# Hybrid decoder layer on one core: the head of its z stage with a plain fp32 first product

## The chip, the cores and the metric

The kernel runs on one core of a Trainium2 chip. A core has a matrix engine (PE, with PEld for its weight loads), a vector engine (DVE), a scalar engine (ACT), a general engine (POOL), and SyncE (SP), which issues most of the transfers. Each engine works through its own list of instructions in order and waits on semaphores for the others. Matrix products are written to PSUM, a small memory of banks; everything else works in SBUF. The metric is the device time of one execution in microseconds, the median of several.

## The reference

One decoder layer with 1024 tokens of 1024 features in fp32. Cut to what matters here:

```python
h = rms_norm(x, norm1_w)                       # x * rsqrt(mean(x*x) + 1e-6) * norm1_w
proj = h @ w_in                                # 1024 x 3592
da_q, da_k, da_v, dn_qkv, dn_z, dn_a, dn_b = split(proj)
...                                            # differential attention; gated DeltaNet, times silu(dn_z)
x = x + mix @ w_out
h = rms_norm(x, norm2_w)
x = x + square(relu(h @ w_up)) @ w_down
```

The columns of `dn_z` (512), `dn_a` and `dn_b` (4 each) are computed first. They are the 520 columns from 3072 on, and this is what the text calls the z stage.

## The kernel before, in words

The program runs through these stages: norm and z; the DeltaNet's projections with their preparation; its scan together with the attention's projections; attention; output projection; and the two products of the MLP, which use a scheme of seven products in place of eight.

Almost every product is made in three passes. An fp32 operand is split into a rounded part H (type fp32r, which PE reads faster) and the remainder L. Then H·H, H·L and L·H are added up. A split costs one ACT copy (rounding) and one DVE subtraction (remainder). `hH` and `hL` hold the split, normalised and turned input for the whole first half of the program; the function `nat` makes one product from them, 8 blocks of the inner dimension with 3 matmuls each (lines 206, 207 and 208 in `mm3`).

The z stage works on 8 row blocks (`tb`) of 128 tokens and 2 weight units (`u`) of 260 columns. For each row block:

- `z_square` makes the sum of squares on ACT (two halves for block 0), then the root on DVE and POOL (`rstd`, lines 231 and 232).
- `z_scale` multiplies x by the root and by norm1_w on DVE. The row norm1_w was spread over all 128 partitions at the start by a matmul with ones; this is an fp32 matmul without a split.
- `z_turn` transposes 4 of the 8 column blocks on PE into a PSUM tile; `h_round` (ACT) and `h_rest` (DVE) split that tile into `hH` and `hL`.
- `z_mm` is the product with one weight unit, into one of two buffers of the pool `pj`. `z_gate` reads it: tanh on ACT, a multiply on DVE (L300), a multiply with the norm weight on POOL, a store. The DVE instruction is the last reader of the PSUM buffer for unit 0.

Each weight unit comes in four raw quarters `wraw` of 260 KB. `z_round` (ACT) and `z_rest` (DVE) split one quarter. The transfers stand on SP in the order of the text: x of block 0 in two halves, the four quarters of unit 0, x of block 1, the four quarters of unit 1, a norm weight, x of blocks 2 to 7.

In the z stage the order of PE, DVE and ACT is written out by hand (`manual_schedule`). The first four products are block 0 with unit 0, block 1 with unit 0, block 0 with unit 1 and block 1 with unit 1. As `pj` has two buffers, the third product waits until the gate has read the first. In the hand order that gate stands behind the splits of both units and behind the root of block 2. All other order, and that of SP and POOL, is set by a scheduler; a planner with costs for each engine (`Interleave`) arranges later stages.

Of the kernel before, what the change touches and what calls it, by code (L numbers as in the profile page):

```python
# [13 lines left out]
ALU = mybir.AluOpType  # L14
# [107 lines left out]
def tile_hymba_layer(  # L122
# [140 lines left out]
    def z_unit(u):  # L263

        ops = [staged(t).rearrange("p (k c) -> p k c", k=KB) for t in ("wH", "wL")]
        raws = []
        for k in range(0, KB, 2):
            raw = n1.tile([P, 2 * UC], F32, tag="wraw", name="wraw", bufs=8).rearrange("p (k c) -> p k c", k=2)
            nc.sync.dma_start(raw, w_in_v[:, k:k + 2, 3072 + UC * u:3072 + UC * (u + 1)])
            raws.append(raw)  # L270
        return ops, raws

    xts = [n1.tile([P, DM], F32, tag="xt", name="xt", bufs=NT) for _ in range(NT)]
    w1r = n1.tile([P, DM], F32, tag="hn", name="w1r", bufs=2)[0:1, :]
    nc.scalar.dma_start(w1r, norm1_w)
    cuts = (slice(0, 512), slice(512, 1024))
    for c in cuts:
        nc.sync.dma_start(xts[0][:, c], x2[0:P, c])
    wz = [z_unit(0)]
    nc.sync.dma_start(xts[1], x2[P:2 * P, :])  # L280
    wz.append(z_unit(1))
    dnw4 = n1.tile([P, 4, P], F32, name="dnw4")
    nc.sync.dma_start(dnw4[:, 0], dn_out_norm_w.partition_broadcast(P))
    for tb in range(2, NT):
# [5 lines left out]
    def z_mm(tb, u):  # L290
        ps = pj.tile([P, 512], F32, tag="pj", name="ps_z")
        nat(ps[:, :UC], tb, wz[u][0], 0, UC)
        return ps

    def z_gate(tb, u, ps):
        n = UC if u == 0 else 252
        th = n1.tile([P, UC], F32, tag="zth", name="zth", bufs=2)
        S.activation(th[:, :n], ps[:, :n], AF.Tanh, scale=0.5)
        zg = n1.tile([P, UC], F32, tag="zg", name="zg", bufs=4)
        last = V.scalar_tensor_tensor(zg[:, :n], th[:, :n], 1.0, ps[:, :n], ALU.add, ALU.mult)  # L300
        G.tensor_tensor(zg[:, :n], zg[:, :n], dnw4[:, UC * u:UC * u + n], ALU.mult)
        if u == 1:
            last = V.tensor_copy(ab[:, tb, :], ps[:, 252:260])
        nc.sync.dma_start(zg_d[tb, :, UC * u:UC * u + n], zg[:, :n])
        return last

    def z_round(u, i):
        S.copy(wz[u][0][0][:, 2 * i:2 * i + 2], wz[u][1][i])

    def z_rest(u, i):  # L310
        wh, wl = [x[:, 2 * i:2 * i + 2] for x in wz[u][0]]
        V.tensor_tensor(wl, wz[u][1][i], wh.bitcast(F32), ALU.subtract)
# [1 line left out]
    hns_, turned_ = {}, {}  # L314

    def z_square(tb, parts=1):

        sq = n1.tile([P, DM], F32, tag="nsq", name="nsq", bufs=1)
        ss = n1.tile([P, 2], F32, tag="nss", name="nss", bufs=2)
        for i in range(parts):  # L320
            c = cuts[i] if parts > 1 else slice(0, DM)
            S.activation(sq[:, c], xts[tb][:, c], AF.Square, accum_out=ss[:, i:i + 1])
# [4 lines left out]
        hns_[tb] = n1.tile([P, DM], F32, tag="hn", name="hn", bufs=2), r  # L327

    def z_scale(tb, c):
        hn, r = hns_[tb]  # L330
        return V.scalar_tensor_tensor(hn[:, c], xts[tb][:, c], r, w1b[:, c], ALU.mult, ALU.mult)

    def z_turn(tb, g):
        ps = pt_.tile([P, 512], F32, tag="pt", name="ps_tr")
        for j in range(4 * g, 4 * g + 4):
            last = T.transpose(ps[:, (j % 4) * P:(j % 4 + 1) * P], hns_[tb][0][:, j * P:(j + 1) * P], ident)
        turned_[tb, g] = ps.rearrange("p (k t) -> p k t", k=4)
        return last

    def h_round(tb, g):  # L340
        return S.copy(hH[:, 4 * g:4 * g + 4, tb * P:(tb + 1) * P], turned_[tb, g])

    def h_rest(tb, g):
        ks, sl = slice(4 * g, 4 * g + 4), slice(tb * P, (tb + 1) * P)
        V.tensor_tensor(hL[:, ks, sl], turned_[tb, g], hH[:, ks, sl].bitcast(F32), ALU.subtract)

    ones = gp.tile([P, P], F32, name="ones")
    with tc.manual_schedule(engines={T.engine, V.engine, S.engine}):


        V.memset(ones, 1.0)
        pw = pm.tile([P, 512], F32, tag="pm", name="ps_w")
        for i in range(6):
            T.transpose(pw[:, 0:P], ident, ident)
        pws = []
        for c in cuts:
            ps = ph.tile([P, 512], F32, tag="ph", name="ps_w1")
            T.matmul(ps, ones[0:1, :], w1r[:, c], start=True, stop=True)
            pws.append(ps)
        for i in range(6):  # L360
            T.transpose(pw[:, 0:P], ident, ident)
        V.tensor_copy(w1b[:, cuts[0]], pws[0])
        z_square(0, 2)
        V.tensor_copy(w1b[:, cuts[1]], pws[1])
        z_round(0, 0)
        for g in range(2):
            z_scale(0, cuts[g])
            z_turn(0, g)
            h_round(0, g)
            if g == 0:  # L370
                z_round(0, 1)
                z_rest(0, 0)
                h_rest(0, 0)
        z_rest(0, 1)
        h_rest(0, 1)
        for i in (2, 3):
            z_round(0, i)
            z_rest(0, i)
        banks0 = {0: z_mm(0, 0)}
        z_square(1)  # L380
        z_scale(1, slice(0, DM))
        z_round(1, 0)
        z_rest(1, 0)
        for g in range(2):
            z_turn(1, g)
            h_round(1, g)
            h_rest(1, g)
            z_round(1, 1 + g)
            z_rest(1, 1 + g)
        banks0[1] = z_mm(1, 0)  # L390
        z_round(1, 3)
        z_rest(1, 3)
# [11 lines left out]
        z_square(3)  # L404
        z_gate(0, 1, banks0[2])
        z_scale(3, slice(0, DM))
        z_gate(1, 1, banks0[3])
        for tb in range(2, NT):
            ps = z_mm(tb, 0)
            if tb + 1 < NT:  # L410
                marks = [z_turn(tb + 1, 0), z_turn(tb + 1, 1)][1:]
                for g in range(2):
                    marks += [h_round(tb + 1, g)]
                    h_rest(tb + 1, g)
            marks += [z_gate(tb, 0, ps)]
            if tb + 2 < NT:
                z_square(tb + 2)
                z_scale(tb + 2, slice(0, DM))
# [1321 lines left out]
```

## Time and profile before

| | |
|---|---|
| median of 3 runs | 1268.11 us (1265.73 to 1270.84) |
| the profiled execution | 1264.09 us, of which the profile's span is 1262.1 us |
| PE busy | 1234.1 us, 98% |
| DVE busy | 817.8 us, 65% |
| ACT busy | 614.0 us, 49% |
| instructions | 18992 |

In the lines that follow, a row of the timeline has the start, the duration, the engine, the line of the kernel, the operation and its tiles, a count, and in brackets the idle time of that engine ahead of it and what ended it. Rows of busy time by windows have their columns named where they stand. Times count from the start of the span. The duration of a matmul in these rows includes its way through the array; matmuls that follow each other start closer together than their duration.

### The profile page before, as it was taken

To read this page: it belongs to the slowest core of one execution; us is meant where nothing else is said; L and a number is where in the kernel's file an instruction comes from. 1 tells how busy PE (TensorE), PEld (TensorE's weight loads), DVE (VectorE), ACT (ScalarE), POOL (GpSimd) and SP (SyncE) were. 2 spreads that over 40 slices of the span, in tenths; PEclk is the share of its full clock that TensorE was granted. 3 is DMA by queue.
4 is the path that set the end of the run, shared out by engine and by line. 5 is a ranking of instruction groups with operands and counts; after the bars stand their busy time and mean duration, and the time that the engine had idled before them with its cause. 6 is when DMAs were issued, how large, how long until landed. Compare 5 with 4: busy or idle time off the path is not lost.

```text
span 1262.1 us, 18992 instructions
## 1 busy us (share of the span) xinstructions
PE 1234.1 (98%) x6973; PEld 1061.5 (84%) x6973; DVE 817.8 (65%) x1416; ACT 614.0 (49%) x1237; POOL 111.0 (9%) x141
## 2 busy tenths in 40 slices
PE   8999999999999999998999999999999999999998
PEld 7988888899998998887887888888887788888887
DVE  6557797557657647776589555665566865687553
ACT  4469554334446545665557444554554333333331
POOL 2211110022212300011200000000000000000000
PEclk9999999999999999999999999999999999999999
DMA  6135554368858656334246534534368755433311
GB/s 240 39 94 144 142 165 118 82 191 260 258 144 245 168 179 162 99 91 143 94 147 207 191 136 167 183 134 144 124 226 323 302 200 200 167 101 100 128 39 67
DMA packets 165814, 200.02 MB, mean 158 GB/s; under 512 B 20905, under 2 KB 126169, under 8 KB 165722
## 3 DMA queue, kind: packets, MB, share of 16 engines
q1 hardware_dynamic: 165720, 198.82, 48.8%
q8 instruction: 55, 0.90, 0.3%
q14 instruction: 37, 0.30, 0.1%
q10 hardware_dynamic: 2, 0.00, 0.0%
HBM read 132.71 MB, written 66.06 MB: 157 GB/s over the span
## 4 chain that ended last, share of the span: by engine, by line
PE 85%; DMA 8%; DVE 3%; ACT 2%; issue 1%; SPq 1%; POOLq 0%; DVEq 0%; POOL 0%; ACTq 0%
PE X L1368 4%; PE X L1367 4%; PE X L1366 4%; PE ps_qk L941 4%; PE ps_qk L942 4%; PE ps_qk L943 4%; PE X L1662 3%; PE X L1663 3%; PE X L1661 3%; PE ps_dn L206 3%; PE ps_dn L207 3%; PE ps_dn L208 3%; PE Y L1366 2%; PE Y L1367 2%; PE Y L1368 2%; PE ps_o L1109 2%
## 5 line engine op out<-in xcount | busy, mean ns | idle before, releaser
L1285 ACT CAST hH<-ur 128x1024 fp32r<-128x1024 f32 x56 | 58.6, 1050 | 175.6 <-PE Z L1662 85.2
L1286 DVE TENSOR_TENSOR hL<-ur,hH 128x1024 fp32r<-128x1024 f32 x56 | 68.3, 1222 | 82.4 <-ACT hH L1285 82.3
L941 PE MATMUL ps_qk<-wH,hH 128*128 128x256 f32 x384 | 114.8, 299 | 0.1
L942 PE MATMUL ps_qk<-wL,hH 128*128 128x256 f32 x384 | 108.5, 283 | 0.0
L943 PE MATMUL ps_qk<-wH,hL 128*128 128x256 f32 x384 | 108.4, 282 | 0.0
L1286 DVE TENSOR_TENSOR op<-raw,op 128x1024 fp32r<-128x1024 f32 x48 | 58.7, 1223 | 74.2 <-PE X L1367 39.5
L1662 PE MATMUL X<-hL,hH 128*128 128x512 f32 x224 | 87.4, 390 | 2.7 <-DVE hL L1286 2.7
L1661 PE MATMUL X<-hH 128*128 128x512 f32 x224 | 87.5, 391 | 1.4 <-DVE b L1563 1.4
L1663 PE MATMUL X<-hH,hL 128*128 128x512 f32 x224 | 87.3, 390 | 0.0
L206 PE MATMUL ps_dn<-hH,wH 128*128 128x512 f32 x192 | 76.2, 397 | 0.3 <-ACT cp L561 0.3
L208 PE MATMUL ps_dn<-hH,wL 128*128 128x512 f32 x192 | 76.0, 396 | 0.0
L207 PE MATMUL ps_dn<-hL,wH 128*128 128x512 f32 x192 | 75.7, 395 | 0.0
L941 PEld LDWEIGHTS ps_qk<-wH,hH 128*128 128x128 f32 x384 | 73.5, 191 | 0.3 <-ACT qn L960 0.2
L942 PEld LDWEIGHTS ps_qk<-wL,hH 128*128 128x128 f32 x384 | 73.5, 191 | 0.0
L943 PEld LDWEIGHTS ps_qk<-wH,hL 128*128 128x128 f32 x384 | 73.2, 191 | 0.0
L1286 DVE TENSOR_TENSOR hL<-dw,hH 128x1024 fp32r<-128x1024 f32 x56 | 68.0, 1217 | 3.2 <-ACT hH L1285 3.2
L1285 ACT CAST op<-raw 128x1024 fp32r<-128x1024 f32 x48 | 50.4, 1052 | 36.9 <-PE Y L1368 19.9
L1285 ACT CAST hH<-dw 128x1024 fp32r<-128x1024 f32 x56 | 58.5, 1047 | 14.8 <-PE Z L1663 8.1
L565 DVE SCALAR_TENSOR_TENSOR cy<-cp,pv,cy 128x512 f32<-128x512 f32 x72 | 53.6, 745 | 13.1 <-ACT cy L563 12.4
L201 DVE TENSOR_TENSOR wL<-wraw,wH 128x512 fp32r<-128x512 f32 x64 | 43.8, 697 | 27.8 <-ACT wH L200 27.5
L200 ACT CAST wH<-wraw 128x512 fp32r<-128x512 f32 x64 | 38.2, 621 | 43.2 <-DMA wraw<-in_w_in_dram 28.5
L1070 ACT ACTIVATE pexp<-ps_sc,mx 128x128 f32<-128x128 f32 (+7 forms) x64 | 47.4, 741 | 22.9 <-DVE mx L1066 22.6
(354 smaller groups left out, 3459.8 us busy)
## 6 DMA issues: line engine op xcount, KB each, us to landing
ur<-ud SPq DMA_DIRECT2D x28, 1024.0 KB, 5.1
raw<-in_w_up_dram SPq DMA_DIRECT2D x32, 512.0 KB, 3.9
dw<-in_w_down_dram SPq DMA_DIRECT2D x32, 512.0 KB, 7.3
wraw<-in_w_in_dram SPq DMA_DIRECT2D x48, 256.0 KB, 2.9
qk_d<-qa SPq DMA_DIRECT2D x32, 256.0 KB, 3.6
ud<-ua SPq DMA_DIRECT2D x16, 512.0 KB, 2.6
ud<-s SPq DMA_DIRECT2D x16, 512.0 KB, 2.7
pka<-park_d SPq DMA_DIRECT2D x32, 192.0 KB, 3.8
```

The source lines that it names most:

```text
L206: T.matmul(ps, lh(k), rh(k), start=(k == 0), stop=False)
L207: T.matmul(ps, lh(k), rl(k), start=False, stop=False)
L208: T.matmul(ps, ll(k), rh(k), start=False, stop=(k == n - 1))
L941: T.matmul(ps[:, :256], hH[:, k, sl], wh[:, k, :], start=(k == 0), stop=False)
L942: T.matmul(ps[:, :256], hH[:, k, sl], wl[:, k, :], start=False, stop=False)
L943: T.matmul(ps[:, :256], hL[:, k, sl], wh[:, k, :], start=False, stop=(k == KB - 1))
L1285: S.copy(dst[0], src)
L1286: V.tensor_tensor(dst[1], src, dst[0].bitcast(F32), ALU.subtract)
L1366: T.matmul(ps, op[0][:, k, cs], h[0][:, k, :], start=start and k == 0, stop=False, skip_group_check=True)
L1661: T.matmul(bank[t], v[0][:, j, sl], v[2][:, j], start=s0, stop=False, skip_group_check=True)
L1662: T.matmul(bank[t], v[0][:, j, sl], v[3][:, j], start=False, stop=False, skip_group_check=True)
L1663: T.matmul(bank[t], v[1][:, j, sl], v[2][:, j], start=False, stop=s1, skip_group_check=True)
```

## The change

Four things change, all in the z stage.

1. The first product (block 0, unit 0) no longer uses the split operands. Block 0's turned tiles are copied whole to a new fp32 tile `hF`, and 8 plain fp32 matmuls multiply `hF` with the raw weight quarters. The split of block 0 into `hH` and `hL` is made later, from `hF`, between the weight splits of unit 1, for the third product.
2. The transfer of x of block 1 is issued ahead of the four quarters of unit 0. Block 1 is squared and scaled early, and its 8 transposes stand between the fourth and the fifth matmul of the first product.
3. The splits of unit 0 are made for the second product; all but the first quarter's stand behind the rounding of block 1.
4. `z_square` is parted into `z_square` (the sum of squares) and `z_root`. The squares themselves, which nobody reads, go into the tile that later holds the scaled x, and their own tile is gone. norm1_w is loaded into a row of `hF`.

```diff
-    w1r = n1.tile([P, DM], F32, tag="hn", name="w1r", bufs=2)[0:1, :]
+    hF = n1.tile([P, KB, P], F32, name="hF")
+    w1r = hF.rearrange("p k c -> p (k c)")[0:1, :]
...
-    wz = [z_unit(0)]
     nc.sync.dma_start(xts[1], x2[P:2 * P, :])
-    wz.append(z_unit(1))
+    wz = [z_unit(u) for u in range(2)]
...
         V.tensor_copy(w1b[:, cuts[0]], pws[0])
         z_square(0, 2)
+        z_root(0, 2)
         V.tensor_copy(w1b[:, cuts[1]], pws[1])
-        z_round(0, 0)
+        z_square(1)
         for g in range(2):
             z_scale(0, cuts[g])
+            if g == 0:
+                z_root(1)
             z_turn(0, g)
-            h_round(0, g)
...
+            S.copy(hF[:, 4 * g:4 * g + 4, :], turned_[0, g])
         z_scale(1, slice(0, DM))
+
+        ps = pj.tile([P, 512], F32, tag="pj", name="ps_z")
+        banks0 = {0: ps}
+        for k in range(KB):
+            if k == 4:
+                z_turn(1, 0)
+                z_turn(1, 1)
+            T.matmul(ps[:, :UC], hF[:, k, :], wz[0][1][k // 2][:, k % 2, :], start=k == 0, stop=k == KB - 1)
+        z_round(0, 0)
+        z_round(0, 1)
+        z_rest(0, 0)
+        for g in range(2):
+            h_round(1, g)
+            h_rest(1, g)
+            z_round(0, 2 + g)
+            z_rest(0, 1 + g)
+        z_rest(0, 3)
         z_round(1, 0)
         z_rest(1, 0)
         for g in range(2):
-            z_turn(1, g)
-            h_round(1, g)
-            h_rest(1, g)
+            ks = slice(4 * g, 4 * g + 4)
+            S.copy(hH[:, ks, 0:P], hF[:, ks, :])
+            V.tensor_tensor(hL[:, ks, 0:P], hF[:, ks, :], hH[:, ks, 0:P].bitcast(F32), ALU.subtract)
             z_round(1, 1 + g)
             z_rest(1, 1 + g)
         banks0[1] = z_mm(1, 0)
         z_round(1, 3)
         z_rest(1, 3)
         z_square(2)
+        z_root(2)
         z_gate(0, 0, banks0[0])
```

More of the change, by code (lines that the diff above doesn't have):

```diff
@@ L316, in z_square @@
     def z_square(tb, parts=1):
-        sq = n1.tile([P, DM], F32, tag="nsq", name="nsq", bufs=1)
+        hn = n1.tile([P, DM], F32, tag="hn", name="hn", bufs=2)
         ss = n1.tile([P, 2], F32, tag="nss", name="nss", bufs=2)
@@ L321, in z_square, with z_root @@
             c = cuts[i] if parts > 1 else slice(0, DM)
-            S.activation(sq[:, c], xts[tb][:, c], AF.Square, accum_out=ss[:, i:i + 1])
+            S.activation(hn[:, c], xts[tb][:, c], AF.Square, accum_out=ss[:, i:i + 1])
+        hns_[tb] = hn, ss
+    def z_root(tb, parts=1):
+        hn, ss = hns_[tb]
         if parts > 1:
@@ L326, in z_square @@
         rstd(r, ss[:, 0:1], 1.0 / DM, EPS, n1, "nrt", 1)
-        hns_[tb] = n1.tile([P, DM], F32, tag="hn", name="hn", bufs=2), r
+        hns_[tb] = hn, r
     def z_scale(tb, c):
@@ L363, in tile_hymba_layer @@
         z_square(0, 2)
+        z_root(0, 2)
         V.tensor_copy(w1b[:, cuts[1]], pws[1])
-        z_round(0, 0)
+        z_square(1)
         for g in range(2):
             z_scale(0, cuts[g])
+            if g == 0:
+                z_root(1)
             z_turn(0, g)
-            h_round(0, g)
[L370 to L380, printed above, removed]
-        z_scale(1, slice(0, DM))
+            S.copy(hF[:, 4 * g:4 * g + 4, :], turned_[0, g])
+        z_scale(1, slice(0, DM))
+        ps = pj.tile([P, 512], F32, tag="pj", name="ps_z")
[14 more added lines that the diff above has]
+        z_rest(0, 3)
         z_round(1, 0)
@@ L404, in tile_hymba_layer @@
         z_square(3)
+        z_root(3)
         z_gate(0, 1, banks0[2])
@@ L417, in tile_hymba_layer @@
                 z_square(tb + 2)
+                z_root(tb + 2)
                 z_scale(tb + 2, slice(0, DM))
```

## The prediction

> **What bounds the kernel now.** I read three views in this order: the page, to see which engine the whole program leans on; busy time by windows, to see where that engine is not full; the timeline of the first 25 us, to see what it waits for there.
>
> ```profile
> span 1262.1 us, 18992 instructions
> PE 1234.1 (98%) x6973; PEld 1061.5 (84%) x6973; DVE 817.8 (65%) x1416; ACT 614.0 (49%) x1237; POOL 111.0 (9%) x141
> ```
>
> PE, the matrix engine, is busy for 98% of the span, so a microsecond that it waits at the head is a microsecond of the kernel, unless a later wait swallows it.
>
> ```profile
> 0.00:5.00 5.00, 3.46 (x9) 2.10 (x10) 0.25 (x3) 2.62 (x5) 1.87 (x11) 1.00 0.57 174
> 5.00:10.00 5.00, 4.34 (x13) 2.07 (x11) 2.88 (x7) 1.26 (x4) 0.55 (x1) 1.00 1.02 333
> ...
> 20.00:25.00 5.00, 4.78 (x40) 4.56 (x40) 4.73 (x8) 2.58 (x6) 1.30 (x2) 1.00 0.21 60
> 25.00:30.00 5.00, 5.00 (x44) 5.00 (x44) 2.58 (x6) 2.78 (x6) 1.97 (x3) 1.00 0.49 160
> 30.00:40.00 10.00, 10.00 (x86) 9.83 (x85) 4.96 (x10) 3.21 (x7) 2.72 (x5) 1.00 0.14 44
> ```
>
> The columns are the stretch, its length, then busy time (and count) of PE, its weight loads, DVE, ACT and POOL, the granted clock, the DMA share and GB/s. From 25 us on PE has no gap (5.00 of 5.00, 10.00 of 10.00). DVE is nearly full in 20 to 25 (4.73 of 5.00). So the question is only when the gapless stretch begins. The timeline has it:
>
> ```profile
> 1.54 1.54 PE L354 MATMUL ps_w<-ident 128*128 128x128 f32 x6 [1.54 <-POOL ident masks.py:199]
> ...
> 6.18 0.62 ACT L308 CAST wH<-wraw 128x520 fp32r<-128x520 f32 x1 [1.17 <-DMA wraw<-in_w_in_dram]
> ...
> 7.43 0.74 DVE L331 SCALAR_TENSOR_TENSOR hn<-xt,nr,w1b 128x512 f32<-128x512 f32 x1
> ...
> 8.22 1.12 PE L336 MATMUL ps_tr<-ident,hn 128*128 128x128 f32 x4
> 9.38 0.59 ACT L341 CAST hH<-ps_tr 128x512 fp32r<-128x512 f32 x1 [2.57 <-PE ps_tr L336]
> ...
> 10.00 0.69 DVE L345 TENSOR_TENSOR hL<-ps_tr,hH 128x512 fp32r<-128x512 f32 x1 [1.22 <-ACT hH L341]
> ...
> 13.18 0.69 DVE L345 TENSOR_TENSOR hL<-ps_tr,hH 128x512 fp32r<-128x512 f32 x1 [1.23 <-ACT hH L341]
> ...
> 14.09 1.05 ACT L322 ACTIVATE nsq<-xt 128x1024 f32<-128x1024 f32 x1
> ...
> 15.27 0.15 DVE L231 TENSOR_SCALAR nrt<-nss 128x1 f32<-128x1 f32 x1
> ...
> 16.12 1.28 DVE L331 SCALAR_TENSOR_TENSOR hn<-xt,nr,w1b 128x1024 f32<-128x1024 f32 x1 [0.70 <-DMA xt<-in_x_dram]
> ...
> 18.22 0.59 ACT L341 CAST hH<-ps_tr 128x512 fp32r<-128x512 f32 x1 [2.46 <-PE ps_tr L336]
> ...
> 18.84 0.69 DVE L345 TENSOR_TENSOR hL<-ps_tr,hH 128x512 fp32r<-128x512 f32 x1 [0.82 <-ACT hH L341]
> ...
> 19.44 0.69 DVE L312 TENSOR_TENSOR wL<-wraw,wH 128x520 fp32r<-128x520 f32 x1
> ...
> 20.05 0.68 DVE L345 TENSOR_TENSOR hL<-ps_tr,hH 128x512 fp32r<-128x512 f32 x1
> ...
> 20.65 1.30 DVE L312 TENSOR_TENSOR wL<-wraw,wH 128x520 fp32r<-128x520 f32 x2
> ...
> 21.95 0.15 DVE L231 TENSOR_SCALAR nrt<-nss 128x1 f32<-128x1 f32 x1
> ...
> 22.23 0.43 DVE L300 SCALAR_TENSOR_TENSOR zg<-zth,ps_z 128x260 f32<-128x260 f32 x1
> ...
> 22.71 0.39 PE L206 MATMUL ps_z<-wH,hH 128*128 128x260 f32 x1 [0.23 <-DVE zg L300]
> ```
>
> The last row is the one that matters. The third product (block 0, unit 1) starts at 22.71 because the accumulators have two buffers and it reuses the first one, which DVE releases by its gate instruction `zg` (L300) at 22.23. From there PE never stops. That gate stands on DVE behind all splits of both weight units. I call the start of the third product S: S before is 22.71, and the change is worth what it moves S by. What PE gains ahead of S, it only waits away.
>
> DVE has the same instructions ahead of that gate in both kernels: three scalings, eight weight remainders (L312), four remainders of h (L345) and the two small root steps of blocks 1 and 2. So S moves only by DVE's idle time between them, of which the rows show 1.22, 1.23, 0.70 and 0.82 us before.
>
> **The change, part by part.** *Up to the first turn* nothing on the path moves: block 0's x still is first in the queue, so DVE scales at 7.43, PE turns at 8.22 and ACT copies at 9.38. That copy now is a plain copy to hF (same 128x512, 0.59). In the old trace the next engine took up such a copy at 10.00, 0.62 after it began. So the first plain product starts at 10.0 instead of behind the splits, for the old one stood at 12.17:
>
> ```profile
> 12.17 0.57 PE L206 MATMUL ps_z<-wH,hH 128*128 128x260 f32 x1
> 12.53 0.42 PE L207 MATMUL ps_z<-wL,hH 128*128 128x260 f32 x1
> 12.75 0.42 PE L208 MATMUL ps_z<-wH,hL 128*128 128x260 f32 x1
> ...
> 16.69 0.28 PE L206 MATMUL ps_z<-wH,hH 128*128 128x260 f32 x1
> 16.81 0.28 PE L207 MATMUL ps_z<-wL,hH 128*128 128x260 f32 x1
> ...
> 17.55 1.07 PE L336 MATMUL ps_tr<-ident,hn 128*128 128x128 f32 x8 [0.34 <-DVE hn L331]
> ```
>
> *Price of the plain product.* Old matmuls follow each other at 0.216 us at first (12.53 to 12.75) and at 0.12 later (16.69 to 16.81), though the clock column says 1.00 throughout: PE runs at half pace until about 16.3, 4.1 us after its first product matmul. The one plain fp32 matmul of this kernel is the broadcast of norm1_w:
>
> ```profile
> L358 PE MATMUL ps_w<-w1r,ones x4: 1056/1056/1217, 3.0 to 5.7; 1*128 1x512 f32 x4
> ```
>
> Two instructions leave four records, 0.90 us apart ((5.7 - 3.0) / 3) for 512 columns at half pace. For 260 columns that is 0.457 a record, and two old sweeps (2 x 0.216) give 0.43: I take 0.44, so 0.88 a matmul, half of it at full pace. Eight take 7.0 us at half pace against 24 x 0.216 = 5.2 for the old product. The first four, ahead of block 1's turn, take 3.5 (3.45 to 3.66): 10.0 to 13.5.
>
> *Turn of block 1 inside the product.* ACT took up a turned group 1.16 us after PE began it at half pace (8.22 to 9.38) and 0.67 after at full pace (17.55 to 18.22). If the pace rises 4.1 us after the first dense matmul, as before, it does so at 14.1, and 0.6 us of the four transposes' 1.12 lie ahead of that. I take 1.1, nearest to the half-pace row: ACT rounds the first group at 14.6 (bounds 14.17 and 14.8). In the old kernel this point is 18.22.
> The Trainium skill, "TensorE: Matmul & The Clock Gate", Part 1, says that the clock starts at half and doubles after one busy window of some 3.4 us. By that the pace would rise at 13.4, ACT would round at 14.2 and S would come 0.4 earlier than mine; the trace's own 4.1 us is used.
>
> *DVE from there.* The first h remainder follows 0.62 later (18.22 to 18.84). Behind it are queued eleven subtractions instead of the old five, because the split of unit 0 is moved behind the turn (only its first quarter lies ahead): four of h and seven of weights. Five took 18.84 to 21.95, 0.622 each; eleven take 6.84. The plain operands hF come from SBUF rather than PSUM; the weight remainders do too, and their rows are as long (0.69), so no extra price. Then 0.28 from the root step to the gate (21.95 to 22.23) and 0.48 from the gate to PE (22.23 to 22.71).
>
> ACT must keep ahead of this:
>
> ```profile
> 18.70 0.63 ACT L308 CAST wH<-wraw 128x520 fp32r<-128x520 f32 x1
> ...
> 19.23 0.59 ACT L341 CAST hH<-ps_tr 128x512 fp32r<-128x512 f32 x1
> ...
> 19.70 1.16 ACT L308 CAST wH<-wraw 128x520 fp32r<-128x520 f32 x2
> ...
> 20.76 1.07 ACT L322 ACTIVATE nsq<-xt 128x1024 f32<-128x1024 f32 x1
> ```
>
> Its copies start 0.51 apart (five in 18.22 to 20.76), faster than DVE's 0.622; ten of them and block 2's square end 6.3 us after the turn (5.1 and the 1.2 of a square with its sum, below), and the tanh 0.4 later, while DVE comes to the gate after 7.74. The two extra ACT copies to hF are ahead of the turn, while ACT has nothing else: nothing. That lead of 1.0 is what hides them; were it gone, every copy more would cost its 0.51.
>
> *Sum:* S = 14.6 + 0.62 + 6.84 + 0.28 + 0.48 = 22.82, against 22.71: +0.1 us (by the bounds of the turn, 14.17 and 14.8, -0.3 to +0.3). DVE begins its chain 3.6 us earlier (15.2 for 18.84) but has six more subtractions in it (3.7 us). The idle time has only moved: DVE now stands still from about 12.2 to 15.2, while the first plain half is computed.
>
> *x of block 1 ahead of the weights.* In the first 5 us 870 kB land (174 GB/s), then 333 kB a us. Both blocks of x (1049 kB) are there at 5.5 by bytes. But the first weight quarter, 790 kB down the old queue and thus due at 4.5, was taken up only at 6.18: a lag of up to 1.6. So block 1 lands between 5.5 and 7.1. Its square and sum take 1.2 (14.09 to 15.27), and its root step stands on DVE between the two scalings of block 0, in a slot at 8.1 (7.43 + 0.66): 6.7 to 8.3 against 8.1, so 0 to 0.2, taken as 0. It costs more beyond that, see below. The first weight quarter (1315 kB) then lands by 6.3 to 7.9, and PE wants it at 10.0: hidden by 2 us. On SP the issue of x goes ahead of four weight issues, all done before their bytes can move; the other issues stay. On POOL the root of block 1 goes ahead of the norm-weight steps, whose result is first needed at the gate: nothing.
>
> *Rest.* Squares written into hn instead of a buffer of their own: hn of that block isn't written before. The root split off from the square has the same neighbours from block 2 on. The order of every engine behind the third product is unchanged, so nothing later moves but by S. All together: 1264.09 + 0.1 = 1264.2 by this execution's own time. The median of the runs shown, 1268.11, is 4.0 higher than it, so my figure for the median is 1268.2.
>
> **Rivals.**
> *Slower: PE falls back to half pace in the new wait.* The turn ends at about 14.7, four more plain matmuls at 0.44 take it to 16.5, and the second product ends at 19.4 (24 x 0.12 = 2.9); then PE waits for the gate until 22.8, 3.4 us, where the old wait is 0.23. Where the pace rises late, the second product ends at up to 21.6 and only 1.2 remain. For it: PE ran at half pace at 12.5 after standing still and turning. Against: no row shows it fall back once full. Price: the third product at 0.216 instead of 0.12, 24 x 0.096 = 2.3 us: 1270.5. It decides once that wait is long enough to count as idle; it could then happen on every execution. The same page and section of the skill put that at an idle window of some 3.4 us that runs free of the kernel; no trace here shows it, and a wait of 3.4 would rarely cover a whole one.
> *Faster: the pace rises inside the first plain half*, because four sweeps without a break count sooner than the old product's first matmuls. At 12.5 the half ends 0.5 earlier and the turn runs at full pace: ACT rounds at 13.7, S = 21.9, 0.8 before the old one: 1267.3. For it: the rise in the old trace isn't tied to a count. Against: 7.8 us of transposes and one-row matmuls from 1.54 on did not raise it.
> *Slower: block 1 lands late.* Its root stands in front of the second scaling, so past 6.9 every us of landing delays the plain product by one: at 8.0 it is +1.1, 1269.3. For it: the 1.6 us lag. Against: x rows came without such a lag.
> *No rise before the second product:* it then takes 5.2 from 18.7 and ends at 23.9; S is 1.2 later: 1269.3. The old rise came 4.1 us into dense work; here 8.7 us lie ahead.
>
> **How the numbers follow.** Forecast 0.60; fall back 0.15; early rise 0.13; late landing 0.06; late rise 0.03; something outside the head 0.03, of either sign. The runs spread from 1265.73 to 1270.84 (0.2% each way), more than any case, so the range is these cases plus the runs: low 1264.09 - 0.8 = 1263.3, high 1270.84 + 0.7 = 1271.5. 0.5% is 6.3 us, about what a measurement of this kernel can tell from no change; no case reaches it, so only the last 0.03 and a part of the fall back (if it repeated) go outside: faster 0.02, same 0.95, slower 0.03.
>
> **What would show it.** The plain product's first record at 10.0, 16 records 0.44 apart at first; ACT's first round of block 1 at 14.6; eleven subtractions on DVE without a gap from 15.2; the second product ended near 19.4 to 21.6 and the third waiting for DVE `zg` until 22.8; full PE from there. It is wrong if PE's third product starts more than 1 us off that, if its first matmuls are 0.216 apart, or if the splits read hF at another price than 0.69.

## The result, and the profile after

The changed kernel takes 1271.02 us in the median of 20 runs (1264.87 to 1278.2) against 1266.85 us for the kernel before (1263.77 to 1270.95, also 20 runs). The ratio is 1.0029, with a 95% interval of 1.0017 to 1.0040. A second set of runs of the same two kernels gave 1.0035 (1.0018 to 1.0052). So the change costs 0.3%, some 4 us: less than the 0.5% within which the prediction had put it, yet a loss that both intervals keep clear of nothing, and forty times the 0.1 us that the prediction's sum had.

The profiled execution of the changed kernel has a span of 1266.2 us and a time of 1267.95 us, 4.1 us of span more than before. The page of the changed kernel, in its lines for the span, the busy time of each engine and three of the DMA queues:

```profile
span 1266.2 us, 18974 instructions
PE 1235.3 (98%) x6965; PEld 1063.1 (84%) x6965; DVE 816.8 (65%) x1416; ACT 615.3 (49%) x1239; POOL 111.2 (9%) x141
...
q1 hardware_dynamic: 165720, 198.82, 48.9%
q8 instruction: 55, 0.90, 0.3%
q14 instruction: 37, 0.30, 0.1%
```

PE is as busy as before, but it has 8 matmuls and 8 weight loads fewer (6965 for 6973 each). The columns of the queue lines are packets, MB and share. Queue 8 carries instructions: 55 packets that are 0.90 MB together, thus 16 kB each. 0.90 MB over PE's 13,930 records are 65 bytes a record, so they are taken here for PE's own program, fetched while it runs, some 250 records at a time. That line was on the page of before too, and the prediction passed over it. Whose instructions queue 14 carries is not shown.

The timeline of the changed kernel's head answers to the prediction's last steps. Only the rows that answer to a step are shown:

```profile
7.50 1.06 ACT L321 ACTIVATE hn<-xt 128x1024 f32<-128x1024 f32 x1 [2.54 <-DMA xt<-in_x_dram]
...
8.68 0.15 DVE L231 TENSOR_SCALAR nrt<-nss 128x1 f32<-128x1 f32 x1 [0.51 <-ACT hn L321]
...
10.39 1.92 PE L385 MATMUL ps_z<-wraw,hF 128*128 128x260 f32 x8
...
12.15 1.04 PE L340 MATMUL ps_tr<-ident,hn 128*128 128x128 f32 x8
12.78 0.59 ACT L345 CAST hH<-ps_tr 128x512 fp32r<-128x512 f32 x1 [0.56 <-PE ps_tr L340]
13.02 1.92 PE L385 MATMUL ps_z<-wraw,hF 128*128 128x260 f32 x8
...
13.40 0.69 DVE L349 TENSOR_TENSOR hL<-ps_tr,hH 128x512 fp32r<-128x512 f32 x1 [0.97 <-ACT hH L345]
...
17.58 0.28 PE L208 MATMUL ps_z<-wH,hL 128*128 128x260 f32 x1
...
20.41 0.14 DVE L231 TENSOR_SCALAR nrt<-nss 128x1 f32<-128x1 f32 x1
20.47 0.41 DVE L300 SCALAR_TENSOR_TENSOR zg<-zth,ps_z 128x260 f32<-128x260 f32 x1
...
20.93 0.58 PE L206 MATMUL ps_z<-wH,hH 128*128 128x260 f32 x1 [3.08 <-DVE zg L300]
...
21.53 0.42 PE L208 MATMUL ps_z<-wH,hL 128*128 128x260 f32 x1
21.75 0.42 PE L206 MATMUL ps_z<-wH,hH 128*128 128x260 f32 x1
...
24.17 0.28 PE L206 MATMUL ps_z<-wH,hH 128*128 128x260 f32 x1
24.29 0.28 PE L207 MATMUL ps_z<-wL,hH 128*128 128x260 f32 x1
```

Half of the plain product takes 1.92 us here, where the prediction had 3.5. The turn of block 1 stands at 12.15, ACT rounds it at 12.78, and the eleven subtractions run from 13.40 to 20.41. The third product, whose start the prediction calls S, begins at 20.93, which is 1.8 us ahead of before. (In four other executions with the same order up to there, S was 21.05 to 21.94.) But PE has stood still for 3.08 us ahead of it, and it then runs at 0.216 a matmul until about 24, when it goes back to 0.12. Busy time by windows of the same kernel shows it in the clock column, the third from the right:

```profile
15.00:20.00 5.00, 2.86 (x24) 2.65 (x22) 5.00 (x9) 4.65 (x10) 0.60 (x2) 1.00 0.98 393
20.00:25.00 5.00, 4.07 (x22) 4.07 (x23) 2.96 (x5) 0.00 (x0) 2.02 (x3) 0.66 0.21 59
```

0.66 is a mean over full and half pace. From 25 us on, the same piece of PE's work stands 0.4 us earlier than before. So in this execution the head has gained, and the whole loss arises later.

Where that is can be worked out by pairing the matmuls of two executions by their order and subtracting their start times. This table is worked out so from the traces (us by which PE is behind before, in the stretch that begins at that time; three of the kernels are experiments of the next section):

```
stretch   after  before_minus8  after_shift8  gate_shift8
  40       -0.4      -0.4           1.6          -1.8
 240       -1.0      -1.2           0.9          -1.9
 260       -0.2      -0.6           0.8          -2.0
 360        0.0       0.3           1.6          -1.7
 380        0.8       1.2           1.7          -1.9
 400        3.4       2.4           3.8          -0.9
 960        1.7       2.6           1.7          -2.5
1000        4.2       4.6           1.2          -4.0
```

The changed kernel loses 0.8 us at 254, 0.8 near 375, 2.7 near 400 (of which 1.7 come back by 660) and 2.4 near 998. None of these places was touched.

Part of such a loss is a longer wait, and part is the half pace that can follow it. The windows near 400 and near 1000 us have it in the clock column; first the kernel before:

```profile
395.00:410.00 15.00, 12.10 (x96) 11.09 (x95) 9.80 (x24) 8.56 (x24) 4.04 (x5) 1.00 0.85 248
990.00:1010.00 20.00, 17.34 (x69) 13.87 (x69) 20.00 (x16) 7.27 (x8) 0.00 (x0) 0.91 0.63 243
```
```profile
395.00:410.00 15.00, 10.77 (x76) 10.17 (x75) 8.51 (x20) 7.17 (x19) 3.64 (x4) 0.89 0.78 240
990.00:1010.00 20.00, 15.78 (x59) 12.52 (x58) 20.00 (x16) 7.05 (x7) 0.00 (x0) 0.83 0.84 314
```

It is not this execution alone. The mean granted clock of a run is 0.997 in the median of 35 runs of the kernel before and 0.994 in 12 of the changed one (the runs of after_again, below). 0.003 of 1265 us is 3.8 us, against 4.6 between their medians. So up to that much of the loss is more time at half pace, and what has to be explained is why PE waits longer and then falls back more often.

### The profile page after: what moved, and what is told of

The parts are those of the page before. It is cut to its first block, busy times and chain, and to the rows that moved or that the text cites. A ratio compares the mean times of both kernels' runs of the same rounds, so it can differ in the third digit from the quotient of the medians.

```text
span 1266.2 us, 18974 instructions
## 1 busy us (share of the span) xinstructions
PE 1235.3 (98%) x6965; PEld 1063.1 (84%) x6965; DVE 816.8 (65%) x1416; ACT 615.3 (49%) x1239; POOL 111.2 (9%) x141
## 4 chain that ended last, share of the span: by engine, by line
PE 86%; DMA 8%; DVE 3%; ACT 1%; SPq 1%; issue 1%; DVEq 0%; POOL 0%; ACTq 0%
PE X L1384 4%; PE X L1383 4%; PE X L1382 4%; PE X L1678 4%; PE X L1679 3%; PE X L1677 3%; PE ps_qk L957 3%; PE ps_dn L206 3%; PE ps_qk L959 3%; PE ps_qk L958 3%; PE ps_dn L208 3%; PE ps_dn L207 3%; PE Y L1384 2%; PE Y L1383 2%; PE Y L1382 2%; DMA wraw<-in_w_in_dram 2%
## 5 line engine op out<-in xcount | busy, mean ns | idle before, releaser
L581 DVE SCALAR_TENSOR_TENSOR cy<-cp,pv,cy 128x512 f32<-128x512 f32 x72 | 53.5, 745 | 11.0 <-ACT cy L579 10.3
L1082 DVE TENSOR_REDUCE mx<-ps_sc 128x1 f32<-128x128 f32 (+7 forms) x64 | 47.6, 754 | 17.2 <-PE ps_sc L1080 17.0
```

## The experiments

Theories, as they stood in the expectations. A: the new wait ahead of the third product, with the half pace behind it, is the whole loss. B: the loss behind the head has nothing to do with the change and varies from run to run. C: the length of PE's program costs something. D, which was formed when A and B had fallen: PE's program is 16 entries shorter (8 matmuls and 8 weight loads), so every later fetch of instructions meets another transfer.

**after_again.** The changed kernel once more.

> The changed kernel once more, for another execution's rows. Theory A (PE's pace falls back to half in the new wait ahead of the third product, and the third product pays for it): the wait of about 3 us ahead of the third product is there again, its first matmuls are 0.216 us apart for 3.4 or 6.8 us, and the ratio to before is about 1.003. Theory B (the loss arises later, where this profile falls behind by 2.6 us near 400 us and by 2.4 near 1000, and the head is innocent): the third product may run at either pace, the head ends no later than before's, and the loss stands again near 400 and 1000 us.

Measured: 1269.61 us against 1264.98, ratio 1.0035 (1.0018 to 1.0052). The loss is real, and not one of the first runs alone. S was 21.7, and PE was at half pace from 22.4 for 3.4 us.

**fill_wait and fill_turns.** PE is given work that nobody reads in the new wait, once products and once transposes.

```diff
         banks0[1] = z_mm(1, 0)
+        for i in range(22):
+            T.matmul(pw[:, :UC], hH[:, 0, P:2 * P], wz[0][0][0][:, 0, :], start=True, stop=True)
```
```diff
         banks0[1] = z_mm(1, 0)
+        for i in range(24):
+            T.transpose(pw[:, 0:P], ident, ident)
```

> The changed kernel with 22 matmuls of 128x260 (2.6 us at full pace) between the second and the third product, into a PSUM tile that nobody reads, so that PE has no long wait. Theory A: the third product starts at about 20.9 with its matmuls 0.12 apart; the head ends some 1.8 us ahead of before's, and the time is 1.4 to 1.8 us below before's (ratio 0.9986 to 0.999). Theory B: the time stays at about 1270.5 (ratio 1.003), filled or not.

> The same filling, but with 24 transposes of the identity (2.6 us at full pace) in place of the matmuls. Theory A, and a transpose counts as work for the pace: like the filling with matmuls, ratio 0.9986 to 0.999. Theory A, and a transpose doesn't count: the third product at 0.216 again and a ratio of about 1.003. Theory B: 1.003 in any case.

Measured: 1260.85 and 1262.31 us against 1264.98, both 0.9976 (0.9962 to 0.9989 and 0.9964 to 0.9987). Busy time by windows, first of the kernel with products, then of the one with transposes:

```profile
20.00:25.00 5.00, 4.81 (x41) 4.60 (x40) 2.99 (x5) 0.44 (x2) 2.02 (x3) 1.00 0.21 48
```
```profile
20.00:25.00 5.00, 4.58 (x40) 4.35 (x39) 3.52 (x6) 0.29 (x2) 2.02 (x3) 1.00 0.23 63
```

The pace stays at 1.00 in both. So the wait itself lets it fall, and transposes hold it as products do. The Trainium skill, "TensorE: Matmul & The Clock Gate", Part 4, says that transposes do not count as work for the pace; this trace does not agree, if its transposes are of the kind that is meant: its rows show them as matmuls with the identity. The head then ends 1.2 to 1.8 us ahead of before. That is less than the 0.6% (1.0035 to 0.9976, some 7.5 us) by which these kernels are faster than the changed one. A does not explain the remaining 5 us. Both also make PE's program longer.

**gate_early.** The gate of the first product moves ahead of the splits of unit 1, so that PE hardly waits.

```diff
         z_rest(0, 3)
+        z_gate(0, 0, banks0[0])
         z_round(1, 0)
...
         z_root(2)
-        z_gate(0, 0, banks0[0])
         z_scale(2, slice(0, DM))
         banks0[2] = z_mm(0, 1)
```

> The changed kernel with the gate of block 0, unit 0 moved ahead of the splits of unit 1 on ACT and DVE, so that the buffer of the third product is free when the second one ends. Theory A: the third product starts at about 18 and goes at the pace of DVE's splits, to about 21.6; PE never waits more than 2 us at a stretch, no half pace, and the time is 2 to 3 us below before's (ratio 0.998). Theory B: about 2 us below the changed kernel, still above before (ratio 1.001 to 1.002).

Measured: 1267.07 us, 1.0015 (0.9998 to 1.0032). Its head ends 1.5 us ahead of before, with no half pace in it, and the kernel is still not faster. Theory A, by which it would have been at 0.998, falls with that: where the wait is gone, a loss of some 3 us stays (2.1 by the medians, and the 1.5 won at the head), though the interval is wide.

**tail_fill, before_again, x1_first.** The first adds 22 small matmuls behind the last product of the changed kernel. The second is the kernel before, unchanged. The third is the kernel before with one part of the change.

```diff
+    for i in range(22):
+        T.matmul(Z[0][:, :64], hH[:, 0, 0:P], hH[:, 0, 0:64], start=True, stop=True, skip_group_check=True)
```
```diff
-    wz = [z_unit(0)]
     nc.sync.dma_start(xts[1], x2[P:2 * P, :])
-    wz.append(z_unit(1))
+    wz = [z_unit(u) for u in range(2)]
```

> The changed kernel with 22 matmuls of 64 columns behind the last product of the program, where PE has nothing left to do and DVE is still adding and storing. The filling of the wait won 7.5 us, though the half pace at the head costs at most 2 to 3: this run tells whether the filling helped by being in the wait, or only by making PE's instruction list longer. Theory A (the wait and the half pace that follows it): nothing changes against the changed kernel, ratio to before 1.003 to 1.0035, half pace at the third product. Theory C (the length or place of PE's instructions sets something in the later stages): much of the 7.5 us is won here too, ratio 0.998 to 1.000.

> The kernel before, against itself, for a second execution's rows. Ratio 1.000 in every theory. Theory A: the third product starts 0.5 us or less after the second one ends and at full pace; half pace shows only in later stages (near 400, 590 and 1000 us), in one or two stretches. Theory B: the later waits of PE (254, 372, 405, 995 us) vary from execution to execution as much as between the kernels, by 1 to 2 us each.

> The kernel before with one part of the change alone: x of block 1 is issued ahead of the four weight quarters of unit 0. By the prediction the transfer is hidden, since the first quarter is wanted only when the first group is turned: ratio 1.000, S within 0.3 us of 22.7. If the lag of the queue is more than 2 us, the first rounding (ACT L308) comes behind its old place by up to 1.6 us and S with it: ratio 1.001.

Measured: 1269.28 us, 1.0033 (1.0016 to 1.0049); 1265.34 us, 0.9999 (0.9982 to 1.0016); 1265.79 us, 0.9997 (0.9980 to 1.0014). The length alone is nothing, since the 22 matmuls at the end change nothing: C falls. A comparison of the kernel before with itself shows no difference, so B's loss from run to run does not explain a ratio of 1.003. And block 1's x ahead of the weights costs nothing that the interval could show. In its profile the third product starts 0.8 us later, where at most 0.3 was expected; 0.8 us is 0.0006 of the time. The row (before: 22.71):

```profile
23.48 0.39 PE L206 MATMUL ps_z<-wH,hH 128*128 128x260 f32 x1 [0.24 <-DVE zg L299]
```

**before_minus8, after_shift8, gate_shift8.** These test D from both sides. The first takes 8 of the 12 idle transposes from the start of the kernel before; nobody reads them, and its head is otherwise the old one. The other two give the changed kernel, and the one with the early gate, 8 matmuls back behind the third product.

```diff
-        for i in range(6):
+        for i in range(4):
             T.transpose(pw[:, 0:P], ident, ident)
...
-        for i in range(6):
-            T.transpose(pw[:, 0:P], ident, ident)
```
```diff
         z_gate(1, 0, banks0[1])
+        for i in range(8):
+            T.matmul(pw[:, :64], hH[:, 0, P:2 * P], wz[0][0][0][:, 0, :64], start=True, stop=True)
         z_turn(2, 0)
```

(In gate_shift8 the 8 matmuls have 260 columns and stand in PE's remaining wait.)

> The kernel before without 8 of the 12 transposes of the identity that keep PE busy ahead of the first turn; PE waits for DVE there in any case, so S stays at 22.7, and every later PE instruction comes 16 earlier in the list, as in the changed kernel. Theory D: ratio 1.002 to 1.003 with an unchanged head, the fetch near 72 us, and the fourth quarter 4 us or more from its issue. Theory A and B: 1.000.

> The changed kernel with 8 matmuls of 64 columns behind the third product, so that the wait and its half pace stay and only the place of PE's later instructions is that of before; they cost at most 0.9 us there. Theory A (all of the loss by the wait and its half pace): ratio 1.0035 to 1.004. Theory D (most of it by the place of the fetches): ratio 1.000 to 1.0015, what is left being the half pace at the head less the earlier start, plus the matmuls added.

> The run with the early gate gained 1.5 us at the head, without a half pace there, and yet lost 3.5 us behind it. PE's instructions are fetched by transfers of 16 KB (55 of them in a run), and the plain product has 8 matmuls and 8 weight loads less, so every later fetch comes at another place of the work. Theory D: a fetch now falls on a transfer that the stage waits for (near 72 us on the last quarters of the first DeltaNet weights, which took 4.1 to 6.0 us from issue to rounding in the four profiles with 16 instructions less, and 2.9 to 3.7 in the five others). This run is the early gate with 8 matmuls of 260 columns in PE's 1.2 us wait ahead of block 2's turn, which puts every later instruction back to its place of before at no cost. Theory D: ratio to before 0.9980 to 0.9990, the fetch near 68 us again, the fourth quarter within 3.7 us of its issue. Theory A and B: the head is as it was, so the ratio stays at 1.0015.

Measured: 1270.97, 1264.79 and 1261.57 us against 1265.56, ratios 1.0044 (1.0030 to 1.0057), 0.9988 (0.9974 to 1.0003) and 0.9966 (0.9954 to 0.9979). The old head without 8 idle transposes, with S at 22.29, is as slow as the changed kernel; and the changed kernel with 8 matmuls that nobody reads has lost its loss. This is the main finding. All three moved the way that D said, and further: it had 1.002 to 1.003, 1.000 to 1.0015 and 0.998 to 0.999. The place that D had named was wrong: between 60 and 80 us, where the weights of 72 us are waited for, before_minus8 loses nothing (it is 0.4 us ahead of before at 60 and 1.2 at 80), and its fourth quarter was rounded 3.9 us behind its issue, where 4 or more was expected. The timelines show what stands behind the finding at two other places. First the kernel before:

```profile
250.22 2.70 SPq L686 DMA_DIRECT2D gb<-fsg_d  x6
254.20 2.05 PE L700 MATMUL ps_h<-W,pb 128*64 128x64 f32 x32 [0.96 <-DVE W L704]
...
949.32 2.29 DVE L1689 TENSOR_TENSOR dw<-dw 128x2048 f32<-128x2048 f32 x1 [1.21 <-DMA dw<-in_w_down_dram]
...
985.88 2.29 DVE L1689 TENSOR_TENSOR dw<-dw 128x2048 f32<-128x2048 f32 x1 [2.63 <-DMA dw<-in_w_down_dram]
994.91 0.50 PE L1662 MATMUL X<-hL,hH 128*128 128x512 f32 x1 [2.66 <-DVE hL L1286]
```

The same instructions in the changed kernel:

```profile
249.24 3.61 SPq L702 DMA_DIRECT2D gb<-fsg_d  x6
254.03 2.05 PE L716 MATMUL ps_h<-W,pb 128*64 128x64 f32 x32 [1.78 <-DVE W L720]
...
953.07 2.29 DVE L1705 TENSOR_TENSOR dw<-dw 128x2048 f32<-128x2048 f32 x1 [3.21 <-DMA dw<-in_w_down_dram]
...
989.19 2.29 DVE L1705 TENSOR_TENSOR dw<-dw 128x2048 f32<-128x2048 f32 x1 [4.19 <-DMA dw<-in_w_down_dram]
998.21 0.80 PE L1678 MATMUL X<-hL,hH 128*128 128x512 f32 x1 [4.22 <-DVE hL L1302]
```

In the kernel before without 8 idle transposes (before_minus8):

```profile
249.07 3.29 SPq L684 DMA_DIRECT2D gb<-fsg_d  x6
253.63 2.05 PE L698 MATMUL ps_h<-W,pb 128*64 128x64 f32 x32 [1.54 <-DVE W L702]
...
954.47 2.29 DVE L1687 TENSOR_TENSOR dw<-dw 128x2048 f32<-128x2048 f32 x1 [3.70 <-DMA dw<-in_w_down_dram]
999.76 0.79 PE L1660 MATMUL X<-hL,hH 128*128 128x512 f32 x1 [4.50 <-DVE hL L1284]
```

And in the changed kernel with 8 matmuls more (after_shift8):

```profile
251.11 2.70 SPq L704 DMA_DIRECT2D gb<-fsg_d  x6
254.96 2.05 PE L718 MATMUL ps_h<-W,pb 128*64 128x64 f32 x32 [0.83 <-DVE W L722]
...
950.96 2.29 DVE L1707 TENSOR_TENSOR dw<-dw 128x2048 f32<-128x2048 f32 x1 [1.18 <-DMA dw<-in_w_down_dram]
996.12 0.80 PE L1680 MATMUL X<-hL,hH 128*128 128x512 f32 x1 [2.21 <-DVE hL L1304]
```

At 250 us SP issues six small reloads of 16 kB (`gb`), for which DVE and then PE wait. A row SPq is the time of the issuing itself. In these four it is 2.70 us where the program is as long as before and 3.3 to 3.6 where it is 16 entries shorter. At 950 DVE waits for the last quarter of `dw`, 1.2 against 3.2 to 3.7 us; from there on each step of that chain is 2 us late, and so are the next loads of `dw` (DVE's wait at 985 grows from 2.63 to 4.19), up to PE's wait of 4.2 at 998. These two places account for 3.2 of the 4.1 us.

That a fetch lies on these transfers is seen by asking for the queues of a short window. In the changed kernel, 249 to 251.5 us:

```profile
q1 hardware_dynamic: 342, 0.21, 27.9%
q8 instruction: 1, 0.02, 2.4%
```

The start of that packet in each trace, against the first of the six reloads, gives an order that holds over 13 executions of 11 kernels (us, worked out from the traces; each fetch takes about 1 us on its engine):

```
fetch starts, relative to first reload   issue of six  DVE waits
0.65 or more ahead (7 executions)            2.70       0.58 to 0.72
0.3 to 0.4 ahead (x1_first, gate_early,
                  gate2_shift8)           3.01 to 3.07  0.91 to 1.03
0.0 (before_minus8)                          3.29       1.30
0.3 to 0.4 behind (after, after_again)    3.60 to 3.61  1.49 to 1.54
```

The length of the program sets this only on the average. Tail_fill has 16 entries fewer up to there, and its fetch came 0.65 us ahead and did no harm; x1_first and gate2_shift8 have the length of before, and theirs came 0.3 to 0.4 ahead. Two executions of the kernel before have it 3.1 and 0.75 us ahead.

At the second place the order is sharper. SP issues four quarters of `dw` there, first in after_shift8 and then in the changed kernel:

```profile
942.82 1.91 SPq L1644 DMA_DIRECT2D dw<-in_w_down_dram  x4
```
```profile
942.91 3.14 SPq L1642 DMA_DIRECT2D dw<-in_w_down_dram  x4
```

Worked out from all 14 traces: in the five executions with 16 entries fewer a fetch starts 0.2 to 0.3 us behind the first of the four, and the second issue takes 1.04 to 1.64 us. In the nine others the fetch starts 0.6 us or more ahead, and the second issue takes 0.41 to 0.42. DVE's wait behind it is 1.7 to 3.7 us in the five and 0 to 1.5 in the nine.

It is not only so at these two places. Of SP's 750 issues in an execution, 37 to 49 overlap a fetch of queue 8 in time. Over the 14 executions 36% of these (220 of 618) took more than 0.8 us, of the others 0.7% (66 of 9882). Beside a packet of queue 14 alone it is 4%. So it is beside a fetch of PE's program that SP's issues are held up, though not each time, and between 660 and 900 us hardly at all (2 of 73).

The place of all 55 fetches in the program, taken against the matmuls beside them, moves with its length. Against the kernel before, the median shift of the fetches is -0.2 to 0.0 us in the five kernels with a program of its length, +1.1 to +1.5 in the five that are 16 entries shorter, and -2.1 and -2.9 in the two with 28 or 32 more. At 950 the shift is +1.7 to +1.8 in all five shorter ones. The shift is not the same at each fetch (+4.1 to +4.8 near 68 us), and single fetches move by 2 us and more between executions of programs of equal length.

**after_mid8.** The changed kernel with its head as it is, and the 8 records put back at 79 us (4 plain fp32 matmuls).

```diff
     T.matmul(ps[:, 32:64], ones, gg, start=True, stop=True)
+    for i in range(4):
+        T.matmul(ps[:, 64:96], ones, gg, start=True, stop=True)
```

> The changed kernel with its head as it is, and four plain fp32 matmuls of 32 columns more (8 records and 8 weight loads) behind the one that sums the decays, at about 79 us; nothing reads their result. From there on PE's list stands where it stood before the change; ahead of it, the first DeltaNet weights at about 72 us included, it stands where the change put it. If the place of the fetches is what costs: the fourth weight quarter at 72 us stays late (rounded 4.0 us or more behind its issue, as in the changed kernel, where before it was 3.0 to 3.7), but the fetch near 249.6 goes back to about 247 and the six reloads at 249 us take 2.7 us on SP's queue instead of 3.6, PE's wait at 254 us is 0.8 to 1.0 us instead of 1.8, that at 373 us is 0.7 to 0.9 instead of 1.55, and that near 998 us 2.0 to 3.0 instead of 4.2; ratio to before 0.998 to 1.002. If the eight matmuls of the run with them at the head helped by what they did there (the pace, the turn of block 2), or if the loss is made at the head and at 72 us: the waits at 254 and 998 us stay at 1.8 and 4.2, ratio 1.003.

Measured: 1266.87 us against 1264.53, 1.0013 (0.9996 to 1.0029). That is inside what D expected, but the interval reaches the 1.0029 of the changed kernel, so the time alone decides nothing. The timeline at the second place is as D has it:

```profile
956.92 2.29 DVE L1707 TENSOR_TENSOR dw<-dw 128x2048 f32<-128x2048 f32 x1 [1.24 <-DMA dw<-in_w_down_dram]
...
1002.13 0.51 PE L1680 MATMUL X<-hL,hH 128*128 128x512 f32 x1 [2.36 <-DVE hL L1304]
```

The first place can't be compared: outside the part whose order is written by hand the planner put the DeltaNet stage between 80 and 300 us in another order, and the wait at 254 does not occur. So this run supports D at 950 to 998 us only.

**gate2_shift8.** The early gate, with the second gate and the fourth product early as well, and 8 small matmuls.

```diff
+        z_gate(0, 0, banks0[0])
         z_round(1, 0)
...
         z_root(2)
-        z_gate(0, 0, banks0[0])
+        z_gate(1, 0, banks0[1])
         z_scale(2, slice(0, DM))
         banks0[2] = z_mm(0, 1)
-        z_gate(1, 0, banks0[1])
+        banks0[3] = z_mm(1, 1)
+        for i in range(8):
+            T.matmul(pw[:, :64], hH[:, 0, P:2 * P], wz[0][0][0][:, 0, :64], start=True, stop=True)
         z_turn(2, 0)
         z_turn(2, 1)
-        banks0[3] = z_mm(1, 1)
```

> The changed kernel with the first gate moved ahead of the splits of unit 1 (as in the two runs with the early gate), the second gate moved ahead of the scaling of block 2, the fourth product moved ahead of the turn of block 2, and 8 matmuls of 64 columns behind it, so that PE's list is as long as before. Theory of the place of the fetches: no loss behind the head, and the head ends 1.5 to 3 us ahead of before, so ratio 0.9955 to 0.998, at or under the 0.9966 of the early gate with 8 matmuls in the wait. If the head were all that counts, it is worth no more than the early gate alone (1.0015).

Measured: 1266.01 us against 1264.53, 1.0006 (0.9992 to 1.0020). A miss: the wait that was removed at 21 us comes back at 30. The timeline, and below it busy time by windows:

```profile
30.17 0.56 PE L206 MATMUL ps_z<-wH,hH 128*128 128x260 f32 x1 [2.66 <-DVE ab L303]
30.52 0.42 PE L207 MATMUL ps_z<-wL,hH 128*128 128x260 f32 x1
```
```profile
30.00:35.00 5.00, 4.83 (x22) 4.86 (x23) 2.17 (x4) 0.00 (x0) 1.46 (x3) 0.50 0.15 52
```

With that wait of 2.66 us PE goes to half pace, and its head ends 3.4 us behind before. Behind the head nothing more is lost, and this agrees with D.

The best of all these is gate_shift8, which is faster than both kernels: 0.9966 of before.

## Why the prediction was right and wrong

The class (within 0.5%) held, and the range did at its upper end, 1271.02 in 1263.3 to 1271.5. That is luck: the cause of the loss is in none of its cases, and the range reaches so far because the slowest single run of before went into it. The sum did not hold: +0.1 us where 4 were measured. By its own steps:

- *The plain product.* Its price was right, and the time of the rise was not. The first half was to run at half pace, 0.44 us a record; here its records are 0.22 apart, which is the prediction's price at full pace, because the pace had risen at 10.3 us. In after_again it rose at 12.2, and the records are 0.43 to 0.44 apart ahead of that and 0.22 behind. Over ten executions with this first product the rise lies at 10.3 to 13.0, not at 14.1. That is the rival "the pace rises inside the first plain half", which had a chance of 0.13 and came in all ten.
- *Block 1's landing.* Off by 0.4 us: ACT took up its x at 7.50, the bound was 5.5 to 7.1, and DVE waited 0.51 for it. The plain product started at 10.39 for 10.0. The rival "block 1 lands late" happened to that extent; in nine other executions ACT took it up at 6.3 to 7.5 and the plain product started at 10.0 to 10.5. That the reordering is otherwise hidden fits the time of x1_first (0.9997), but not its S, 0.8 us later.
- *The eleven subtractions.* Right: no gap, 7.0 us for 6.84.
- *S.* 20.93 in place of 22.82, and in place of the 21.9 of the rival, because ACT rounded block 1 at 12.78 and not at 14.6. With the later rise of other executions S was up to 21.9, as the rival had it.
- *The wait and the half pace.* The rival "PE falls back to half pace in the new wait" (0.15) came too, and its 0.216 a matmul was right. It and the early rise were taken as alternatives; they belong together, since the earlier rise makes the second product end sooner (17.9 for 19.4) and the wait stays long. The third product then lost about 1.4 of the 1.8 us that S had gained: -0.4 at 40 us. In the second profile of the changed kernel the head ended 0.6 us behind before, in the third, with the matmuls at the tail, level with it. So the sum for the head, +0.1, is about right, through two errors that cancel, which is luck again.
- *The step that failed* is this: "The order of every engine behind the third product is unchanged, so nothing later moves but by S." The order is unchanged, but the place in PE's program is not. The diff replaces 24 matmuls by 8, which leave 16 records; the part on the change counted these records for their time and every moved DMA issue for its queue, and did not count that PE's own instructions come by DMA as well, and that their fetches hold up SP's issues (1.64 us for 0.41 at `dw`, 3.61 for 2.70 at the reloads). It lay within the 0.03 of "something outside the head", and that chance was too small.

What stays open: the 2.7 us lost near 400 us. PE's wait there grew from 2.70 to 4.23 us, and a stretch of half pace that before does not have follows it. But after_shift8 loses 2.1 there too, gate_shift8 1.0, and x1_first, which has the length of before, 2.6, so the shorter program is not shown to cause it. Where the loss falls also differs between executions of shorter programs: with the matmuls at the tail, 2.5 us are lost between 60 and 80 us, beside the fetch that is 4.4 us later there, with the early gate 3.7 and in after_again 1.5, while the profiled execution of the changed kernel loses nothing at that place. With the matmuls at the tail nothing is lost at 254 and 1.4 us are won at 998, though the kernel is as slow (1.0033). So the two places shown above account for this execution, and not for every one. Nor was it tried to move a fetch without changing the number of instructions; that the fetch delays SP's issues rests on where the fetches fell in the 14 executions, not on taking one away. Why an issue beside a fetch takes longer is not shown.

## What to carry to other kernels

An edit that changes the number of instructions on a busy engine also moves every later fetch of its program, and in a kernel that waits for transfers a few times this can be worth more than the edit (here 0.4%). So before a small loss is put down to the edit, give back the instructions with idle ones behind it, and take the same number from the old kernel at a place where they do nothing. And when an engine's work is made shorter just ahead of a wait, look whether the longer wait lets the clock fall: here the changed head was 0.9988 of before once the program's length was restored (to 1.0003, so not shown to be faster), and with the gate moved ahead of the wait 0.9966.

## What the runs showed of the hardware that was not expected

- Fetches of PE's program are DMA transfers in the midst of the run: 55 packets of 16 kB in 1266 us. Where one of about 1 us started 0.3 to 0.4 us behind the first of six 16 kB reloads, SP took 3.6 us to issue them and not 2.70; of all issues that overlap a fetch 36% took more than 0.8 us, of the others 0.7%.
- In the head PE fell to half pace with waits of 2.66 to 3.08 us (six executions), and stayed there for 3.4 or 6.8 us. The Trainium skill, "TensorE: Matmul & The Clock Gate", Part 1, puts the fall after at least one idle window of some 3.4 us; here less was enough. The table of the Trainium skill's same page, section "Why this matters for your kernels", warns of gaps over some 3 us, which is nearer. No single length decides it here: after waits of 3.18 us (gate_shift8, at 402.6) and 2.83 (tail_fill, at 999.4) the pace stayed, and in after_again it fell at 83.9 with no wait over 0.7 us near it, where PE was busy for 2.0 of the 3.4 us ahead.
- In the profiled execution of the changed kernel the pace had risen by 10.4 us, when PE had done hardly anything but transposes and four one-row matmuls. In nine others with the same start it rose at 10.6 to 13.0, and with the old head at 16.2 to 17.1 in four. The old head differs in that block 0's second turn follows the first with a gap of 2.06 us and not of 0.22. So transposes seem to count, and gaps of 2 us to keep the pace from rising; the second was not tested by itself.
